# An interleave kernel: a tiny early write moved from the first microseconds to just before the first store

## The chip, the cores and the metric

The kernel runs on one core of one Trainium2 chip. The metric is the device time of one execution in microseconds (us). A ratio is the mean time of one kernel's runs over that of the other's from the same rounds, so it is not quite the ratio of the medians quoted beside it.

## The reference

Two float32 arrays of 32 x 256 x 1024 are interleaved element by element into one of 32 x 256 x 2048:

```python
result[..., 0::2] = x
result[..., 1::2] = y
```

It reads 67 MB, writes 67 MB, and does no arithmetic.

## The kernel before

The flat arrays go through SBUF in eight tiles of 128 partitions x 8192 elements, that is 32 KB per partition and 4 MB per tile. VectorE copies x into the even and y into the odd places of an output tile. SyncE issues the loads, ScalarE the stores, and each of the three pools has two buffers.

```python
zero = wpool.tile([16, 128], fp32, name="zero")
nc.vector.memset(zero, 0.0)
first = dataclasses.replace(of, offset=0, ap=[[2 * WL, 16], [1, 128]])
# ... for each tile; the first x tile is loaded in two halves, the second by ScalarE's queue:
        nc.scalar.dma_start(out=first, in_=zero)      # first tile only
        nc.sync.dma_start(out=ytile, in_=ys)
# ... for each half of the tile:
            nc.vector.tensor_copy(out=otile[:, 0::2], in_=xsub)
            nc.vector.tensor_copy(out=otile[:, 1::2], in_=ysub)
            nc.scalar.dma_start(out=os_, in_=otile)
```

The tiny write puts 512 bytes of zeros at the start of 16 rows of the output. The trace has 16 write packets of 512 bytes, one on each of 16 DMA engines. The first real store writes over them, so its values never matter; only its timing could.

Of the kernel before, what the change touches and what calls it, by code (L numbers as in the profile page):

```python
# [3 lines left out]

# [4 lines left out]


@with_exitstack
def _interleave(
    ctx: ExitStack,
    tc: tile.TileContext,
    x: bass.AP,
    y: bass.AP,
    out: bass.AP,
):
    nc = tc.nc  # L20
    P = 128

    total = 1
    for s in x.shape:
        total *= s

    WL = 8192
    WS = 4096

    xf = x.rearrange("b s d -> (b s d)")  # L30
    yf = y.rearrange("b s d -> (b s d)")
    of = out.rearrange("b s d -> (b s d)")

    fp32 = mybir.dt.float32

    xpool = ctx.enter_context(tc.tile_pool(name="xp", bufs=2))
    ypool = ctx.enter_context(tc.tile_pool(name="yp", bufs=2))
    opool = ctx.enter_context(tc.tile_pool(name="op", bufs=2))

    lwidths = [WL] * (total // P // WL)  # L40
    assert sum(lwidths) == total // P


    wpool = ctx.enter_context(tc.tile_pool(name="wp", bufs=1))
    zero = wpool.tile([16, 128], fp32, name="zero")
    nc.vector.memset(zero, 0.0)  # L46
    first = dataclasses.replace(of, offset=0, ap=[[2 * WL, 16], [1, 128]])

    start = 0
    for lw in lwidths:  # L50
        xtile = xpool.tile([P, WL], fp32, name="xtile")[:, :lw]
        ytile = ypool.tile([P, WL], fp32, name="ytile")[:, :lw]

        xs = dataclasses.replace(xf, offset=start, ap=[[lw, P], [1, lw]])
        ys = dataclasses.replace(yf, offset=start, ap=[[lw, P], [1, lw]])
        if start == 0:

            for q, c in ((nc.sync, 0), (nc.scalar, lw // 2)):
                q.dma_start(
                    out=xtile[:, c : c + lw // 2],  # L60
                    in_=dataclasses.replace(xf, offset=c, ap=[[lw, P], [1, lw // 2]]),
                )
            nc.scalar.dma_start(out=first, in_=zero)
        else:
            nc.sync.dma_start(out=xtile, in_=xs)
        nc.sync.dma_start(out=ytile, in_=ys)

        soff = 0
        while soff < lw:
            width = min(WS, lw - soff)  # L70
            otile = opool.tile([P, 2 * WS], fp32, name="otile")[:, : 2 * width]
            os_ = dataclasses.replace(
                of,
                offset=2 * start + 2 * soff,
                ap=[[2 * lw, P], [1, 2 * width]],
            )
            xsub = xtile[:, soff : soff + width]
            ysub = ytile[:, soff : soff + width]
# [3 lines that stand above are left out]
            soff += width  # L82

        start += P * lw
    assert start == total


def kernel(tc, x, y, out):
    nc = tc.nc
    _interleave(tc, x, y, out)  # L90
    tc.close()
    tc.compile()  # L92


    blocks = nc.main_func.blocks
    for engine in (mybir.EngineType.SP, mybir.EngineType.Activation):
        opening = blocks[0].instructions
        at, moved = next(
            (b, i)
            for b in blocks[1:]  # L100
            for i in b.instructions
            if i.engine == engine and i.opcode == "DMACopy"
        )
        assert not moved.sync_info.on_wait
        body = at.instructions
        body.remove(moved)
        gate = next(
            n
            for n, i in enumerate(opening)
            if i.engine == engine and i.opcode == "Drain"  # L110
        )
        opening.insert(gate, moved)
        at.instructions = body
        blocks[0].instructions = opening




    last = nc.main_func.blocks[-1]
    tail = last.instructions  # L120
    wait = tail[0]
    clear = next(n for n, i in enumerate(tail) if i.opcode == "ISA")
    assert wait.engine == mybir.EngineType.SP and wait.opcode == "Drain"
    assert wait.sync_info.on_wait and not wait.sync_info.on_update
    assert tail[clear].engine == mybir.EngineType.Pool
    last.instructions = [
        copy.replace(wait, engine=mybir.EngineType.Pool)
    ] + tail[clear:]


# [1 line left out]
_INS = ['x', 'y']  # L132
_OUTS = [((32, 256, 2048), 'float32')]


# [23 lines left out]
```

## Time and profile before

| what | value | how to read it |
|---|---|---|
| time | 315.84 us, median of 3 (315.67 to 316.25) | the spread is 0.2% |
| span in the profile | 313.8 us | first to last instruction |
| one 32 KB packet on one engine | 1213 ns | 16 engines side by side |

What bounds the kernel is read from its page in the prediction below. Some readings come from the trace's record of single DMA packets, of which the page gives only sums. There, one packet is one row of a tile (32 KB), on one of 16 engines. I call "excess" what packets take beyond their usual 1213 ns, summed over all engines and divided by 16. Consecutive packet records on an engine overlap by about 4 ns, so durations add up to about 1 us more than the engine's time over the whole run. The excess is hardly touched by that. The record does not name the engine of a packet; it is inferred from each packet starting where another ended.

### The profile page before, as it was taken

Reading aid. Unit: us, or ns where it says so; the run is one execution under the profiler, and the core shown is the slowest. Engines: PE = TensorE matmul, PEld = TensorE weight load, DVE = VectorE, ACT = ScalarE, POOL = GpSimd, SP = SyncE. Lnnn points to the kernel's source line nnn. Section 1 sums busy time; section 2 is a strip of 40 time slices with the busy share of each in tenths; the row PEclk is TensorE's granted clock in tenths of the full one; section 3 lists DMA queues with packets and bytes.
Section 4 is the critical chain, followed back from the end, with each engine's and each line's share of the span. In section 5 each row is a group of like instructions: output and inputs, shape, how many; then the busy total and the mean of one; then the engine's idle time right before and its main releaser. Section 6 shows DMA issues by size and latency. Waiting matters only on the chain.

```text
span 313.8 us, 141 instructions
## 1 busy us (share of the span) xinstructions
DVE 72.8 (23%) x33; POOL 0.2 (0%) x4
## 2 busy tenths in 40 slices
DVE  0523002231022410325003150031501305023500
POOL 0000000000000000000000000000000000000000
DMA  8999999999999999999999999999999999999997
GB/s 343 461 414 388 455 414 455 414 455 414 447 422 447 422 430 439 422 447 418 451 414 455 401 468 401 468 401 464 405 455 414 455 414 455 414 455 414 455 414 334
DMA packets 4784, 134.23 MB, mean 428 GB/s; under 512 B 544, under 2 KB 560, under 8 KB 560
## 3 DMA queue, kind: packets, MB, share of 16 engines
q10 hardware_dynamic: 2480, 69.22, 51.1%
q1 hardware_dynamic: 2304, 65.01, 48.4%
HBM read 67.11 MB, written 67.12 MB: 428 GB/s over the span
## 4 chain that ended last, share of the span: by engine, by line
DMA 83%; DVE 11%; DVEq 1%; issue 0%
DMA out_dram<-otile 76%; DMA ytile<-in_y_dram 7%; DVE otile L80 6%; DVE otile L79 5%; DVEq L92 1%; DVEq L79 0%
## 5 line engine op out<-in xcount | busy, mean ns | idle before, releaser
L79 DVE COPY otile<-xtile 128x4096 f32<-128x4096 f32 x16 | 36.6, 2295 | 184.7 <-DMA out_dram<-otile 174.1
L80 DVE COPY otile<-ytile 128x4096 f32<-128x4096 f32 x16 | 36.6, 2291 | 40.0 <-DMA ytile<-in_y_dram 40.0
L46 DVE MEMSET zero<- 16x128 f32 x1 | 0.2, 165 | 1.0 <-PEq L143 1.0
L143 POOL MEMSET const-bfloat16-1.0<- 128x1 bf16 x1 | 0.1, 101 | 0.0
L143 POOL MEMSET const-uint8-127<- 128x1 uint8 x1 | 0.1, 101 | 0.0
L143 POOL MEMSET const-float32-0.0<- 128x1 f32 x1 | 0.1, 98 | 0.2 <-issue 0.2
L143 POOL MEMSET const-float32-1.0<- 128x1 f32 x1 | 0.1, 98 | 0.0
## 6 DMA issues: line engine op xcount, KB each, us to landing
out_dram<-otile ACTq DMA_DIRECT2D x16, 4096.0 KB, 29.1
ytile<-in_y_dram SPq DMA_DIRECT2D x8, 4096.0 KB, 60.8
xtile<-in_x_dram SPq DMA_DIRECT2D x7, 4096.0 KB, 43.6
xtile<-in_x_dram SPq DMA_DIRECT2D x1, 2048.0 KB, 11.7
xtile<-in_x_dram ACTq DMA_DIRECT2D x1, 2048.0 KB, 13.4
out_dram<-zero ACTq DMA_DIRECT2D x1, 8.0 KB, 14.8
```

Of the source, the lines that this page charges most:

```text
L46: nc.vector.memset(zero, 0.0)
L79: nc.vector.tensor_copy(out=otile[:, 0::2], in_=xsub)
L80: nc.vector.tensor_copy(out=otile[:, 1::2], in_=ysub)
L92: tc.compile()
L143: nc = _bacc.Bacc("TRN2", target_bir_lowering=False, num_devices=1)
```

## The change

The intent is that the tiny write goes out shortly before the first store, with data that is there anyway: the first y tile. It needs no zeros then. It lands in the region of the last tile, so that the first store need not wait for it.

```diff
-    wpool = ctx.enter_context(tc.tile_pool(name="wp", bufs=1))
-    zero = wpool.tile([16, 128], fp32, name="zero")
-    nc.vector.memset(zero, 0.0)
-    first = dataclasses.replace(of, offset=0, ap=[[2 * WL, 16], [1, 128]])
 ...
-            nc.scalar.dma_start(out=first, in_=zero)
         else:
             nc.sync.dma_start(out=xtile, in_=xs)
         nc.sync.dma_start(out=ytile, in_=ys)
+        if start == 0:
+            early = dataclasses.replace(
+                of, offset=2 * (total - P * WL), ap=[[2 * WL, 16], [1, 128]]
+            )
+            nc.scalar.dma_start(out=early, in_=ytile[:16, :128])
```

## The prediction

> **What bounds the kernel now.** I read first the page's engine row, its slices and its DMA queue row.
>
> ```profile
> span 313.8 us, 141 instructions
> DVE 72.8 (23%) x33; POOL 0.2 (0%) x4
> ...
> DMA  8999999999999999999999999999999999999997
> GB/s 343 461 414 388 455 414 455 414 455 414 447 422 447 422 430 439 422 447 418 451 414 455 401 468 401 468 401 464 405 455 414 455 414 455 414 455 414 455 414 334
> ...
> q10 hardware_dynamic: 2480, 69.22, 51.1%
> q1 hardware_dynamic: 2304, 65.01, 48.4%
> HBM read 67.11 MB, written 67.12 MB: 428 GB/s over the span
> ```
>
> VectorE works 23% of the span and is the only engine with real work. The DMA queues' packets fill 51.1 + 48.4 = 99.5% of the 16 engines' span: q10 carries what ScalarE issues (the stores), q1 what SyncE issues (the loads). So the bound is bytes through the DMA engines; the copies are hidden. The alternation of 414 and 455 is the edge of a slice cutting packets, not a rate that changes. Three slices leave the pattern: the first (343), the fourth (388, from 23.5 to 31.4 us) and the last (334).
>
> Next the stretches view, to see what the fourth slice hides; the columns are the stretch, its length, VectorE and GpSimd busy, the clock, the DMA share and GB/s.
>
> ```profile
> 1.00:25.50 24.50, 8.10 (x5) 0.00 (x0) 1.00 1.02 428
> 25.50:30.00 4.50, 1.06 (x1) 0.00 (x0) 1.00 0.98 350
> 30.00:310.00 280.00, 63.60 (x28) 0.00 (x0) 1.00 1.00 433
> ```
>
> From 30 us to nearly the end the rate is 433 GB/s. In one stretch alone, around the first store, it is 350 while the engines still count as busy 0.98. The shortfall is (433 - 350) GB/s x 4.5 us = 374 KB, which at 433 GB/s is 0.86 us. The trace's record of single packets gives the same with less of an edge error: a load packet of 32 KB takes 1213 ns throughout, but on each engine the two that start between 25.8 and 27.7 us take up to 1693 and up to 2046 ns. Summed and divided by 16 engines the excess is 0.78 us. After 30 us the whole excess is 0.004 us. So the DMA engines have three losses that are not bytes: about 1.0 us before the first packet starts, 0.64 us of slow first packets, and this 0.78 us at the first store. The rest, 310.93 us per engine, is packets at their full rate.
>
> Last the timeline of the opening, which shows what stands where.
>
> ```profile
> 0.12 0.38 ACTq L59 DMA_DIRECT2D xtile<-in_x_dram  x1
> ...
> 0.92 0.33 SPq L66 DMA_DIRECT2D ytile<-in_y_dram  x1
> 1.00 0.17 DVE L46 MEMSET zero<- 16x128 f32 x1 [1.00 <-PEq L143]
> 1.20 0.39 ACTq L63 DMA_DIRECT2D out_dram<-zero  x1
> 1.30 0.52 SPq L65 DMA_DIRECT2D xtile<-in_x_dram  x1
> 1.87 0.47 SPq L66 DMA_DIRECT2D ytile<-in_y_dram  x1
> ...
> 22.06 4.49 DVE L80 COPY otile<-ytile 128x4096 f32<-128x4096 f32 x2 [5.85 <-DMA ytile<-in_y_dram]
> 24.39 2.56 ACTq L81 DMA_DIRECT2D out_dram<-otile  x2
> 26.59 0.33 SPq L66 DMA_DIRECT2D ytile<-in_y_dram  x1
> ```
>
> The zeros are issued at 1.20 us behind ScalarE's half of the first x tile. Their packets run at 13.7 to 14.4 us, 27 ns each, and the load packets beside them stay at 1213 ns. Then q10 is empty until the first store, issued at 24.39 us; its first packet starts only at 29.18 us. From there q10 is never empty again.
>
> [...] after 29 us the packets of q1 and q10 take turns on each engine. [...] Here the zeros' completion packets start 1.2 us after their data packets, with one load packet between. [...]
>
> **The change part by part.**
> Removed: one memset of 165 ns on an idle VectorE, worth 0, since its first copy waits for x until 11.72 us. One 8 KB write: per engine one packet of 27 ns and one completion of 9 ns, 0.04 us of engine time.
> Added: the same 8 KB write, the same 0.04 us, now issued when the first y tile has landed (22.04 us). Difference in bytes: none.
> Moved: ScalarE's queue issues it for 0.39 us, ending near 22.5 us, while the first store cannot go before its copy ends at 24.39 us, so the store isn't delayed. The tiny write needs no memset and no copy.
> Waits: the first store loses its wait for the zeros (long landed, worth 0). Now the last tile's first store, issued at 290 us, overwrites the tiny region and waits for a write landed some 260 us before (worth 0). The third y load (issued at 26.59 us) reuses the buffer the tiny write reads, so it must wait for that too. If the tiny write lands near 27 or 28 us, this issue slips by 1 to 2 us; but q1 then still holds the second x tile (lands at 36.10), the second y tile (55.44) and the third x tile (74.82), so a late issue leaves no engine idle, worth 0.
> What can move the time is therefore the 0.78 us alone. By an estimate the tiny write's descriptors reach the engines around 23.3 us (22.5 us plus about 0.65 us, the time from the end of the very first issue to its first packet), roughly 2 us before the store's. It, not the store, will then be what wakes q10 from empty and what ends the long run of loads. Its packet wants the next turn (1.2 us), its completion the turn after, so q10 should still hold its completion when the store's descriptors come. If the slow packets belong to waking the queue or the path for writes, and the wait does not depend on the size of the first packet, they move 2 us earlier and nothing is gained. If a small first packet wakes it without holding up the loads, up to 0.78 us go. The sum: 0 for the bytes, 0 for the waits, and between 0 and -0.78 us for the stall, with a mean I choose at -0.25.
>
> **The rivals.**
> (a) The stall belongs to the first large store, whatever came before: tiny write or not, the two packets per engine stay slow. For it: the zeros passed at 14 us with no stall and did not prevent this one. Against: all later stores start without any, though they are just as large. Time 315.8.
> (b) The stall belongs to q10 being empty: it follows the tiny write to about 24 us. For it: q10 is empty just before and at no later time. Against: at 0.1 us q10 also started from empty, and its first packets at 2.78 us took only some 620 ns for 16 KB, against 611 later. Time 315.8 if all of it is paid again at the tiny write, 315.0 if the small packet hides it.
> (c) The zeros at 14 us had paid for something on the write path, hidden there, and the late tiny write now pays it in the open; or the queue drains between tiny write and store, and both pay. Against: the zeros showed no excess at all. Time 316.2 to 316.6.
> (d) A new wait on the path: the third y load or the last tile's store waits for the tiny write. The depths of q1 above speak against it. It would have to starve the loads; I give it almost nothing.
>
> **Range and chances.** Weights: stall mostly gone 35% (near 315.1), unchanged or moved 45% (near 315.8), more of it 20% (near 316.4). The mean is 0.35 x 315.1 + 0.45 x 315.8 + 0.20 x 316.4 = 315.7; I take 315.6, as placing a write just there looks deliberate. The runs before spread by 0.6 us (315.67 to 316.25), so the range must be wider than the three cases: 314.8 to 316.5. Two per cent is 6.3 us, more than all three losses of the DMA engines together (1.0 + 0.64 + 0.78 = 2.4 us). So faster by 2% would need fewer bytes, and slower by 2% would need the loads starved: 1% each.
>
> **What would show it.** Right: the tiny write issued near 22.1 us in the timeline, the first store still near 24.4 us, the stretch from 30 us on at 433 GB/s, DMA queues near 99.5%, and the span within 0.8 us below 313.8 with the change of it found between 22 and 31 us. The load packets there tell whether the stall went (all 1213 ns), moved to 24 us, or stayed. Wrong: slow packets in both places, an excess anywhere after 30 us, or a first store issued later than 25 us.

0 for the bytes, 0 for the waits and -0.25 us for the stall, added to 315.84 us, come to 315.59, and 315.6 is stated. That the rate can't be raised, on which "faster by 2% would need fewer bytes" rests, stands as my estimate, from no 32 KB packet taking less than 1213 ns in the traces of before and changed. The turns between the queues are measured: from 29 to 284 us, 3772 of 3776 packets in the trace of before, and all 3776 in that of the changed kernel, are followed on their engine by one of the other queue (completions count as packets).

## The result, and the profile after

| | median us | range us | runs |
|---|---|---|---|
| before | 315.64 | 315.44 to 316.25 | 6 |
| changed | 315.58 | 315.48 to 315.73 | 6 |

The ratio is 0.9996 with a 95% interval of 0.9983 to 1.0009: the same time. The predicted 315.6 us and its range hold.

The page of the changed kernel, engine row, rate in slices and queues:

```profile
span 313.7 us, 139 instructions
DVE 72.6 (23%) x32; POOL 0.2 (0%) x4
...
GB/s 334 468 401 402 464 405 455 414 451 418 439 430 430 439 414 455 405 464 401 468 401 468 401 468 401 468 401 468 401 464 405 455 414 451 418 435 435 430 439 334
...
q10 hardware_dynamic: 2480, 69.22, 51.1%
q1 hardware_dynamic: 2304, 65.01, 48.5%
```

The memset is gone (32 VectorE instructions in place of 33), and the queues are as full as before. The fourth slice now reads 402 where it read 388, and the third 401 where it read 414. That looks like a gain in one and a loss in the other, but a slice edge moved across a row of packets. The stretches view, with the same edges as in the prediction, decides it:

```profile
1.00:25.50 24.50, 8.00 (x4) 0.00 (x0) 1.00 1.03 428
25.50:30.00 4.50, 1.00 (x1) 0.00 (x0) 1.00 0.96 351
30.00:310.00 280.00, 63.62 (x28) 0.00 (x0) 1.00 1.00 433
```

The middle stretch still moves only 351 GB/s, against 350 before. The stall is neither gone nor moved: it has the same place and the same size.

The timeline of the opening, with start, duration, engine, line, operation and tiles:

```profile
22.00 0.35 ACTq L67 DMA_DIRECT2D out_dram<-ytile  x1
22.00 4.50 DVE L81 COPY otile<-ytile 128x4096 f32<-128x4096 f32 x2 [5.82 <-DMA ytile<-in_y_dram]
24.33 2.54 ACTq L82 DMA_DIRECT2D out_dram<-otile  x2
28.14 0.33 SPq L59 DMA_DIRECT2D ytile<-in_y_dram  x1
```

The tiny write is issued as the first y tile lands, and the first store at 24.33 us is as early as before (24.39). Only the third y load moved, from 26.59 to 28.14 us, because it must wait for the tiny write, which lands at 28.06 us.

The packets show the order on the engines. The tiny write's packets start from 26.06 us, each 27 ns, and the load packets just ahead of them take 1213 ns, those just behind them up to 1428 ns, which is 0.04 us per engine: the tiny write holds next to nothing up. Its completion packets run at 27.3 to 27.7 us. The load packets that start right then take 1729 to 1889 ns, and the first store's packets follow from 29.21 us. The excess is 0.64 us per engine; in the one trace of before it was 0.78. The slow first packets of the opening differ the other way, 0.64 us before and 0.83 us here, so the two together are 1.42 and 1.47 us.

### The profile page after: what moved, and what is told of

Its sections match the earlier page's. It is cut to its first block, busy times and chain, and to the rows that moved or that the text cites. A ratio compares the mean times of both kernels' runs of the same rounds, so it can differ in the third digit from the quotient of the medians.

```text
span 313.7 us, 139 instructions
## 1 busy us (share of the span) xinstructions
DVE 72.6 (23%) x32; POOL 0.2 (0%) x4
## 4 chain that ended last, share of the span: by engine, by line
DMA 83%; DVE 11%; DVEq 1%; issue 0%
DMA out_dram<-otile 76%; DMA ytile<-in_y_dram 7%; DVE otile L81 6%; DVE otile L80 5%; DVEq L93 1%; DVEq L80 0%
```

## The experiments

Two theories were open. Theory 1 is that the stall belongs to the first large store, or to what begins with it, and the tiny write does nothing. Theory 2 is that a tiny write prepares something that the store would else pay for: a write path, or a queue that has run empty.

**no_tiny: no tiny write at all.**

```diff
-            nc.scalar.dma_start(out=early, in_=ytile[:16, :128])
```

(with `early` itself; this is the changed kernel without its added lines)

> No tiny write at all. Theory 1 (the stall of some 0.7 us per engine belongs to the first large store, and the tiny write does nothing): the time stays within 0.15% of the kernel before, 315.3 to 316.1 us, and the load packets just before the first store are long by 0.6 to 0.8 us per engine, as with either tiny write. Theory 2 (an earlier tiny write opens something on the write path that the first store would else pay for): the time grows by 0.5 to 2 us and the stall at the first store is over 1.2 us per engine.

The median was 315.51 us (315.22 to 315.60, 5 runs) against 315.62, ratio 0.9994 (0.9980 to 1.0007). The excess at the first store was 0.80 us. Theory 2 asked for 0.5 to 2 us more; the interval ends at 0.2 us more, and the excess is not over 1.2 us. So it is out at that size, and no tiny write is needed.

**after_again and no_tiny_again: the same two once more, on one chip in the same rounds.** There is no new edit; they put the three versions side by side.

> The changed kernel once more, with five rounds beside the kernel before and beside the next run. If the tiny write's place is without effect, the ratio is 0.999 to 1.001 and its interval holds 1.

> The kernel without a tiny write once more, same chip and same rounds. If the tiny write does nothing wherever it stands, its ratio to the kernel before is within 0.15% of 1, and it lies within 0.15% of the changed kernel's too. If the tiny write is a small cost or a small help, the three differ by more than that.

The changed kernel had 315.64 us (315.50 to 315.69), ratio 0.9998 (0.9985 to 1.0010). The one without a tiny write had 315.44 us (315.43 to 315.54), ratio 0.9993 (0.9982 to 1.0005). The kernel before had 315.56 us. All three ratios are within the 0.15% stated, though the intervals reach a little beyond it. Without the tiny write the median lies 0.1 us below that of the kernel before in both sets, but both intervals hold 1, so this is no shown gain. The stretch around the first store in no_tiny_again:

```profile
25.50:30.00 4.50, 1.07 (x1) 0.00 (x0) 1.00 0.96 350
```

It is the same 350 GB/s. The excess there in five traces of three kernels is 0.78 (before), 0.64 and 0.73 (changed), 0.80 and 0.68 us (no tiny write). The two traces of one kernel differ by 0.09 and 0.12 us, so the 0.14 us between single traces of before and after is not shown to be more than spread.

**early32k: an early write as large as a store's packet.**

```diff
-                of, offset=2 * (total - P * WL), ap=[[2 * WL, 16], [1, 128]]
+                of, offset=2 * (total - P * WL), ap=[[2 * WL, 16], [1, WL]]
             )
-            nc.scalar.dma_start(out=early, in_=ytile[:16, :128])
+            nc.scalar.dma_start(out=early, in_=ytile[:16, :])
```

> As the changed kernel, but the early write takes a whole row of y (32 KB) from each of 16 partitions, so each engine's early packet is as large as a store's. Theory 1 (first large write is what stalls): the load packets just before the early write, near 24 to 26 us, are long by 0.6 to 0.8 us per engine, and those before the first store are at 1213 ns; the time is that of the changed kernel plus 1.2 us for the half MB, about 316.8 us. If the stall belongs to the first store whatever came before, it stays at the first store; the time is the same.

The 1.2 us, here and for early128p, is an estimate: half a MB (524 KB) at the 433 GB/s of the long stretch.

The single run took 319.47 us, not 316.8. The stretches show where:

```profile
25.50:30.00 4.50, 1.00 (x1) 0.00 (x0) 1.00 0.97 182
30.00:34.50 4.50, 0.00 (x0) 0.00 (x0) 1.00 1.00 422
```

The rate fell to 182 GB/s, because each early packet took 3.1 to 4.2 us in place of 1.2. I put that down to my edit, in which all 16 early rows lie in partitions 0 to 15; the next run tests it. Why such packets take so long, no run here shows. The early packets fill 25.96 to 30.35 us, 4.4 us. So no stall can be read at the early write itself. After it, near the first store's packets at 31.6 us, the excess was only 0.08 us. That would fit a stall paid at the first 32 KB writes, but the long packets hide whether it was.

**early128p: the same half MB over all partitions.** The edit is shown against early32k.

```diff
-                of, offset=2 * (total - P * WL), ap=[[2 * WL, 16], [1, WL]]
+                of, offset=2 * (total - P * WL), ap=[[2 * WL, P], [1, 1024]]
             )
-            nc.scalar.dma_start(out=early, in_=ytile[:16, :])
+            nc.scalar.dma_start(out=early, in_=ytile[:, :1024])
```

> As the changed kernel, with the early write taken as 4 KB from each of all 128 partitions, the same half MB as in the run with 16 whole rows but over all partitions. If that run's very long early packets came of its 16 rows lying on few partitions, they are gone: the time is the changed kernel's plus 1.2 us, 316.5 to 317.1 us. If any write with enough bytes brings on the stall, it lies before the early write, near 24 to 27 us, and the first store has none. If only a full store does, it stays at the first store.

The run took 316.62 us, as expected. This fits the few partitions as what made the run before it so long. The packets are also smaller here, but size alone is not it: 32 KB store packets over all partitions take 1213 ns. The place of the stall came out as I had not expected for a write with this many bytes:

```profile
25.50:34.00 8.50, 1.01 (x1) 0.00 (x0) 1.00 0.99 424
34.00:38.50 4.50, 0.00 (x0) 0.00 (x0) 1.00 0.97 364
38.50:300.00 261.50, 62.94 (x28) 0.00 (x0) 1.00 1.00 433
```

From 26 to 35 us every engine alternates a 4 KB write packet (159 ns) with a 32 KB load packet, and the loads have an excess of 0.01 us. Then the first store's packets begin at 37.5 us, and the load packets just before them have 0.56 us. So eight early writes per engine, directly ahead of the store in the same queue, do not take the stall away, and packets of 4 KB do not bring it on. Whether it is the size of the packets or the small share of writes (one byte in nine here) that spares them, this run does not tell apart.

**wake_load: the store queue woken by loads (a failed edit).** I added half of the second y load to ScalarE's queue, written after the tiny write. The rest of the edit, which gives this tile to the second round and halves SyncE's load of it, is left out here.

```diff
             nc.scalar.dma_start(out=early, in_=ytile[:16, :128])
+            ynext = ypool.tile([P, WL], fp32, name="ytile")
+            nc.scalar.dma_start(out=ynext[:, WS:], in_=...)   # second half of the second y tile
```

> As the changed kernel, but right after the tiny write ScalarE's queue also issues half of the second y load, so that the queue's first large packets after its idle time are loads, and the first store comes behind them near 40 us. If the stall belongs to a second queue starting with large packets, it lies near 26 to 29 us and there is none at the first store. If it belongs to the first large store (the change of direction), there is none near 26 to 29 us and 0.6 to 0.8 us per engine at the first store. Time within 1 us of the kernel before either way.

The load waited for nothing, and the scheduler placed it ahead of the tiny write, as the timeline shows:

```profile
0.92 0.37 ACTq L76 DMA_DIRECT2D ytile<-in_y_dram  x1
...
26.36 0.36 ACTq L74 DMA_DIRECT2D out_dram<-ytile  x1
```

So the queue was not woken by loads, and the run does not test what it was for. Its time was 316.0 us. The first y tile landed at 26.34 us, and the stall moved with the store, to 351 GB/s in the 4.5 us from 29 us on.

**wake_load2: the same question with a load that has to wait.** The second half of the third x load, which waits for a free buffer, goes to ScalarE's queue; there is no tiny write.

```diff
+        elif start == 2 * P * lw:
+            for q, c in ((nc.sync, 0), (nc.scalar, lw // 2)):
+                q.dma_start(
+                    out=xtile[:, c : c + lw // 2],
+                    in_=dataclasses.replace(xf, offset=start + c, ap=[[lw, P], [1, lw // 2]]),
+                )
```

> No tiny write; ScalarE's queue issues the second half of the third x load at about 16 us, so that this queue wakes from empty with large load packets and still holds them when the first store comes. If a second queue's waking holds the loads up, the stall lies at 17 to 21 us and there is none later. If the change from loads alone to loads and stores does, all packets are at their usual duration until the first store's packets start, near 34 us, and the packets just before those are long by 0.6 to 0.8 us per engine.

The timeline and the stretches of this run:

```profile
16.23 0.36 ACTq L59 DMA_DIRECT2D xtile<-in_x_dram  x1
...
25.51 2.57 ACTq L80 DMA_DIRECT2D out_dram<-otile  x2
```

```profile
17.00:31.00 14.00, 4.49 (x2) 0.00 (x0) 1.00 0.99 427
31.50:36.00 4.50, 0.00 (x0) 0.00 (x0) 1.00 1.06 375
```

The queue woke from empty at 19.86 us with 16 KB load packets, and up to 31 us the 32 KB packets have an excess of 0.0001 us. The store was issued at 25.51 us and its packets followed in that queue from 35.11 us on, without its having been empty; the load packets around their start (31.5 to 37.5 us) had 0.92 us, somewhat above the 0.6 to 0.8 expected. So a queue that wakes with loads costs nothing here; going from loads alone to loads and stores does. (The time was 316.40 us against 315.79 in one run each; I did not trace the rest of that difference.)

**one_obuf: a store queue that runs empty again and again.** No tiny write, and one output buffer in place of two.

```diff
-    opool = ctx.enter_context(tc.tile_pool(name="op", bufs=2))
+    opool = ctx.enter_context(tc.tile_pool(name="op", bufs=1))
```

> No tiny write, and one output buffer in place of two, so that a store must land before the next copy and the store queue runs empty 15 times while loads go on. If the stall is paid at each change from loads alone to loads and stores, there are several episodes of 0.6 to 0.8 us per engine, one at each such restart. If it is paid once in a run, there is one, at the first store, and every later packet is at 1213 ns. The time is longer by many us either way, since the engines will also stand idle.

The run took 369.12 us, since the engines now also stand idle. The stretches that end just after a restart of the stores, and one in mixed work:

```profile
30.00:45.00 15.00, 0.00 (x0) 0.00 (x0) 1.00 1.01 435
54.00:58.50 4.50, 0.00 (x0) 0.00 (x0) 1.00 0.99 350
99.00:103.50 4.50, 0.00 (x0) 0.00 (x0) 1.00 0.95 350
144.20:148.70 4.50, 0.00 (x0) 0.00 (x0) 1.00 1.00 350
189.20:193.70 4.50, 0.00 (x0) 0.00 (x0) 1.00 0.97 342
```

The same 350 GB/s, or a little less, is back at each of the four. Each store but the first starts after an empty queue, but those restarts are of three kinds. Counting the first store, seven times stores started out of a run of loads and the loads then went on between them: the last two load packets of each engine before the store had an excess of 0.64 to 0.87 us each time. Six times the loads had run up to that moment but none followed: the first store packets had 0.04 to 0.28 us, averaged over the engines. There the cost lies on the engines whose last load ended right where the store began, with store packets of up to 1962 ns (median 1544); engines that had stood idle for a moment had 1214 to 1391 (median 1218). Three times no load was near: at most 0.01 us in the first packets. Starts from a standstill show an excess too: the first load packets after one had 0.58 to 0.73 us at five such starts in this run, and 0.64 to 0.83 us in the opening of the five traces of before, changed and no tiny write. My expectation had only "one per restart" or "one per run", and it is finer than both. In this run the stall is paid anew each time the engines go from loads alone to loads and large stores in turns, and in part where they go from loads straight to stores.

**first_8k: smaller packets in the first stores.** No tiny write, and the two stores of the first tile are cut into eight DMAs with 8 KB rows.

```diff
-            nc.scalar.dma_start(out=os_, in_=otile)
+            if start < P * lw:
+                for c in range(0, 2 * width, WS // 2):
+                    nc.scalar.dma_start(out=..., in_=otile[:, c : c + WS // 2])
+            else:
+                nc.scalar.dma_start(out=os_, in_=otile)
```

> No tiny write, and the two stores of the first tile go out as eight DMAs with 8 KB rows, so that the packets which first mix with the loads are a quarter as long. If the stall needs full 32 KB store packets, there is no excess near 26 to 30 us, and it appears later, where the second tile's stores begin (near 60 us); the time stays within 0.2% of the kernel before. If the stall belongs to the onset of mixing at any size over 4 KB, it stays near 26 to 30 us. If it vanishes altogether, the time falls by up to 0.6 us, less some 0.2 us for the more packets.

The 0.2 us for more packets can be worked out as an estimate from the trace of before: two 16 KB packets of 611 ns take 9 ns more than one of 32 KB, or 5 ns more after the overlap of 4 ns, and 48 more packets per engine come to 0.24 us.

```profile
25.50:30.00 4.50, 1.03 (x1) 0.00 (x0) 1.00 0.95 379
...
90.50:95.00 4.50, 0.00 (x0) 0.00 (x0) 1.00 1.00 350
```

The first mixing cost about half (0.42 us). The 32 KB store packets began at 79.9 us, later than I expected, while no loads ran; they took turns with loads from about 87 us on. A second stall of 0.85 us came only at about 92 us, in the midst of these turns, on the load packets around the end of the first 32 KB store. The finding of the one-buffer run does not cover that, and its cause stays open. From 31 us on the excess was 1.02 us, so in this trace the two together are more than the one they replace. The trace is of the slowest of the six runs (316.82 us; three took 315.65 to 315.67), so these sizes may not stand for the others. The median time was 315.95 us, ratio 1.0014 (1.0001 to 1.0026): no gain.

## Why the prediction was right, point by point

- **The bound.** Right: 433 GB/s from 30 us on in both kernels, and full queues. (The excess after 30 us that it gives as 0.004 us is 0.0048.) What the three losses left over was bytes, which the change does not touch.
- **Removed, added and moved work.** Right, each term worth 0. The memset and the wait of the first store went without trace, the store was issued 0.06 us earlier, and the third y load slipped by 1.55 us, inside the 1 to 2 us foreseen, with the queue of loads never empty.
- **Rival (a), the stall stays at the first large store.** This is what happened. The objection that I raised against it, that later stores are as large and start with no stall, was mis-read: in both kernels no later store starts out of loads alone, and in the one-buffer run some do and pay.
- **Rival (b), the waking of the queue.** Wrong, by two counts: the tiny write woke the queue with next to no excess (0.04 us), and a load that woke it had none either (0.0001 us in wake_load2).
- **Rival (c), a cost once paid in hiding.** Wrong: with no tiny write nothing more was paid.
- **Rival (d), a new wait on the path.** It exists (the third y load) and costs nothing, as weighed.
- **The step that was off.** "Between 0 and -0.78 us for the stall, with a mean I choose at -0.25" was a choice without a measurement behind it. The medians differ by -0.06 us, and the runs without a tiny write show that the true term is not told from 0. That the number came out so close is luck: 315.6 lay nearer to the new rounds of before (315.64) than the 315.84 I started from. The mechanism foreseen as likeliest, "unchanged or moved" at 45%, is what happened, in its "unchanged" half.
- **A smaller miss.** "Its packet wants the next turn" was too early. The tiny write's first packet started 4.06 us after its issue, not at 23.3 us plus a turn: more load packets went ahead of it (two per engine started between 23.3 us and the tiny write), and why is not shown. It still came ahead of the store, as the argument needed.

What stays open is why going over to alternation costs some 0.7 us once, and why first_8k paid a second time at 92 us. The packet records show that the stall appears on the load packets just before the first large store packet, that it is smaller where no load follows, and that the 4 KB writes of early128p did not bring it on. No run here shows the mechanism.

## What to carry to other kernels

A stall next to a rare event is not thereby caused by what is rare about it: before placing a warm-up access with care, run the kernel without it. Here that one experiment settled the change. Making the suspected event recur, by taking a buffer away, brought the stall back seven times, counting the first; the second stall of first_8k shows that the rule drawn from that is not yet complete. In a kernel whose DMA engines are 99.5% full, look at the packet durations first, since they say how much there is to gain before anything is moved.
